# Moving the recurrence's input loads from SyncE's queue to GpSimd's queue in a two-layer FoX / RWKV-7 trunk

## The chip, the cores and the metric

The kernel runs on one core of one Trainium2 chip. The metric is the device time of one execution in microseconds (us). Times come from several runs of the same program; beside them stands one profiled execution, whose trace gives the start and length of each instruction on each engine: TensorE (PE, with its weight loads as PEld), VectorE (DVE), ScalarE (ACT), GpSimd (POOL) and SyncE (SP). SP computes nothing here. It only issues DMA transfers, one after the other, and an issue whose wait is not yet fulfilled holds up all issues behind it.

## The reference, cut to what matters

Input and output are 1024 tokens by 1024 channels in float32. Layer 0 is a forgetting attention with a pooling mixer and a SwiGLU feed-forward (FFN). Layer 1 is an RWKV-7 time mixing and another SwiGLU FFN. The change touches only the recurrence of layer 1:

```
r = (xr @ w_r); k = (xk @ w_k); v = (xv @ w_v)
w = -softplus(-(w0 + tanh(xw @ w1) @ w2)) - 0.5
a = sigmoid(a0 + (xa @ a1) @ a2);  g = sigmoid(xg @ g1) @ g2
kk = heads(k * k_k); kk = kk / max(|kk|, 1e-12)
k = k * (1 + (a - 1) * k_a);  decay = exp(-exp(w))
for each token:                      # 16 heads, a 64 x 64 state each
    sa = state @ (-kk)
    state = state * decay + sa (kk * a)^T + v k^T
    y = state @ r
y = groupnorm(y) * ln_w + ln_b + sum(r * k * r_k) * v
out = (y * g) @ w_o
```

## The kernel before

Activations lie transposed: 128 channels on the partitions, 512 tokens (one "half") along the row, so one tile is 128x512 float32, 256 KB. Every large product is computed with both operands split into a rounded high part and a low rest, as three matmuls (L163 to L165). A weight chunk is therefore loaded raw (`wraw`, L150, issued by SP), cast to its high part by ACT (`whi`, L151), and DVE subtracts to get the low part (`wlo`, L152). There are two raw buffers (`k.rawbufs` is 2), so a raw load waits until the `wlo` of the chunk two places back is done.

The dense part of RWKV (`dense`, L811) computes r, k, v, s (the argument of the decay), a and g of each block of 128 channels and spills them to DRAM through ACT's queue (L799). Four "jobs" then run the recurrence: `job(grp, half)` (L983) takes four channel blocks ("pairs", as each holds two heads) of one half. Its parts are:

- the preparation, for each of the four pairs: load s, k, a, r, v (L1004, L1019, L1034, L1043, L1048, all through `load`, L955), build the factors on DVE and ACT, and multiply on PE (L1025, L1056, L1070, L1081). r, multiplied, is stored to DRAM as c (L1049);
- a triangular solve on DVE (L1092 to L1116: transposes, then 30 steps of L1106 and L1108) and PE (L1126, L1136); POOL's small fills (`ep` L1007, `XR` L1091, `nu` L1100) and copies (`Pc` L1017) belong to it;
- the recurrence over eight chunks of 64 tokens (L1151 to L1189). Beside it `bonus` (L973) loads c and v again and stores b;
- the end, for each pair: load b and g (L1214, L1215), normalise, store y (L1220).

That makes 36 loads a job: 20 + 8 + 8, and 144 in the four jobs. All go into one ring of seven tiles, `ld` (`rw.ld_bufs` is 7), so a load waits for the last reader of the tile loaded seven places earlier.

Beside the jobs runs a filler that keeps PE busy: while jobs (0,0) and (1,0) run, it is the second half's FFN of layer 0; while jobs (0,1) and (1,1) run, it is the first half's FFN of layer 1 (the matmuls `fm`). `weave` (L217) interleaves the two when the program is written. The order in which instructions stand in each engine's queue is then fixed at build time by a scheduler, which places instructions by priority and by its own model of when inputs are ready. At run time every engine takes its queue strictly in that order.

In the profiled execution job (0,0) prepares from about 1047 to 1125 us, job (1,0) from 1270 to 1357, job (0,1) from 1775 to 1862 and job (1,1) from 1998 to 2089.

Of the kernel before, what the change touches and what calls it, by code (L numbers as in the profile page):

```python
# [113 lines left out]
def nm(k, s):  # L114
    k.uid += 1
    return f"{s}_{k.uid}"
# [625 lines left out]
class Rwkv:  # L742
# [211 lines left out]

    def load(self, n):  # L955
        t = self.cp.tile([P, HN], F32, tag="ld", name=nm(self.k, "ld"), bufs=self.ld_bufs)
        self.k.nc.sync.dma_start(t, self.dt(n))
        return t

    def await_(self, n):  # L960
# [591 lines left out]
```

## Time and profile before

| | us |
|---|---|
| median of 3 runs | 2701.37 |
| lowest and highest run | 2699.15 and 2703.07 |
| the profiled execution | 2699.03 |
| span of its trace, first to last instruction | 2697.2 |
| mean granted TensorE clock | 0.993 of full speed |
| bytes moved by DMA | 307 MB, 114 GB/s on average |

The profile has a page (busy time of each engine, the chain of work that ended last, groups of instructions) and views that answer questions about a stretch: who waited for whom, busy time by stretch, instructions in order of time. In a row of the timeline stand start, length, engine, line, operation, output and inputs, and in brackets the idle time before it with what ended it. "SPq" is SP's queue of DMA issues. In the order of time, SP's row shows an issue, not the transfer.

### The profile page before, as it was taken

The numbers are of one execution on the slowest core, as the hardware profiler recorded it, in microseconds if no ns is written. First come the engines' busy times: TensorE is split into PE (matmuls) and PEld (weight loads), VectorE is DVE, ScalarE is ACT, GpSimd is POOL, SyncE is SP. The second block draws the span as 40 slices with busy tenths as digits, with TensorE's granted clock in tenths as the row PEclk, the third lists the DMA queues.
The fourth block names the chain that finished last, engine by engine and source line by source line (L and its number), as shares of the span: only waits on it lengthen the run. The fifth ranks groups of instructions, "written<-read, shape, count | busy, mean of one in ns | idle before, by whom it ended". The sixth has DMA issues, their size and how long they took to land.

```text
span 2697.2 us, 40269 instructions
## 1 busy us (share of the span) xinstructions
PE 2633.8 (98%) x15368; PEld 2080.5 (77%) x15368; DVE 1724.3 (64%) x2940; ACT 1301.9 (48%) x2299; POOL 50.6 (2%) x139
## 2 busy tenths in 40 slices
PE   8999999999999999999999999999999999999999
PEld 6787878788888777777777677777777778888887
DVE  8777684654446655975995685469768856634443
ACT  7555564442224765534634466664445444332232
POOL 1000000000001000000000000000000000000000
PEclk9999999999999999999999999999999999999999
DMA  4111131233333546424523534454344336333333
GB/s 136 58 52 55 44 98 48 83 97 96 96 98 114 168 162 191 129 82 123 160 87 100 194 101 161 160 182 128 91 141 134 93 100 199 109 98 94 98 98 94
DMA packets 170817, 307.03 MB, mean 114 GB/s; under 512 B 18928, under 2 KB 25968, under 8 KB 170624
## 3 DMA queue, kind: packets, MB, share of 16 engines
q1 hardware_dynamic: 156800, 279.29, 33.6%
q10 hardware_dynamic: 13824, 25.17, 2.5%
q8 instruction: 120, 1.97, 0.3%
q14 instruction: 73, 0.60, 0.1%
HBM read 257.96 MB, written 46.43 MB: 113 GB/s over the span
## 4 chain that ended last, share of the span: by engine, by line
PE 77%; DVE 14%; DMA 3%; ACT 3%; issue 2%; SPq 0%; DVEq 0%; ACTq 0%
PE mm L163 16%; PE mm L164 16%; PE mm L165 16%; PE fm L163 6%; PE fm L164 5%; PE fm L165 5%; DVE wlo L152 2%; PE mm L175 1%; DVE nu L1108 1%; DVE pd L1106 1%; DMA wraw<-in_wu_dram 1%; DVE ZL L1064 1%; ACT whi L151 1%; PE o L1173 1%; PE s L1161 1%
## 5 line engine op out<-in xcount | busy, mean ns | idle before, releaser
L151 ACT CAST whi<-wraw 128x512 fp32r<-128x512 f32 x738 | 453.7, 617 | 867.4 <-PE mm L164 478.7
L152 DVE TENSOR_TENSOR wlo<-wraw,whi 128x512 fp32r<-128x512 f32 x738 | 501.3, 684 | 449.6 <-ACT whi L151 441.1
L163 PE MATMUL mm<-hh,whi 128*128 128x512 f32 x864 | 344.1, 400 | 6.2 <-ACT hh L355 6.1
L165 PE MATMUL mm<-hh,wlo 128*128 128x512 f32 x864 | 338.4, 392 | 0.0
L164 PE MATMUL mm<-hl,whi 128*128 128x512 f32 x864 | 337.9, 392 | 0.0
L163 PE MATMUL mm<-uh,whi 128*128 128x512 f32 x728 | 283.6, 391 | 0.9 <-DVE x L1317 0.9
L165 PE MATMUL mm<-uh,wlo 128*128 128x512 f32 x728 | 283.1, 390 | 1.0 <-DVE wlo L152 1.0
L164 PE MATMUL mm<-ul,whi 128*128 128x512 f32 x728 | 283.2, 390 | 0.0
L163 PE MATMUL fm<-h1h,whi 128*128 128x512 f32 x528 | 220.2, 417 | 14.8 <-DVE sg L726 9.9
L164 PE MATMUL fm<-h1l,whi 128*128 128x512 f32 x528 | 210.3, 398 | 0.1
L165 PE MATMUL fm<-h1h,wlo 128*128 128x512 f32 x528 | 209.5, 397 | 0.5 <-DVE wlo L152 0.5
L163 PEld LDWEIGHTS mm<-hh,whi 128*128 128x128 f32 x864 | 162.3, 188 | 43.4 <-ACT hh L355 7.8
L165 PEld LDWEIGHTS mm<-hh,wlo 128*128 128x128 f32 x864 | 162.5, 188 | 34.4 <-issue 0.2
L164 PEld LDWEIGHTS mm<-hl,whi 128*128 128x128 f32 x864 | 162.7, 188 | 33.1 <-DVE hl L260 1.7
L163 PE MATMUL fm<-hh,whi 128*128 128x512 f32 x416 | 170.9, 411 | 3.3 <-ACT hh L259 2.3
L164 PE MATMUL fm<-hl,whi 128*128 128x512 f32 x416 | 164.9, 396 | 0.2 <-DVE hl L260 0.2
L165 PE MATMUL fm<-hh,wlo 128*128 128x512 f32 x416 | 164.6, 396 | 0.0
L163 PEld LDWEIGHTS mm<-uh,whi 128*128 128x128 f32 x728 | 136.5, 188 | 34.6 <-issue 3.5
L164 PEld LDWEIGHTS mm<-ul,whi 128*128 128x128 f32 x728 | 136.6, 188 | 30.9 <-issue 1.1
L165 PEld LDWEIGHTS mm<-uh,wlo 128*128 128x128 f32 x728 | 136.7, 188 | 30.1 <-DVE wlo L152 1.8
L705 DVE TENSOR_TENSOR x<-mm,x 128x512 f32<-128x512 f32 x96 | 66.3, 692 | 119.3 <-PE mm L165 119.2
L163 PEld LDWEIGHTS fm<-h1h,whi 128*128 128x128 f32 x528 | 100.6, 191 | 47.1 <-DVE sg L726 12.2
(338 smaller groups left out, 4645.4 us busy)
## 6 DMA issues: line engine op xcount, KB each, us to landing
wraw<-in_wg_dram SPq DMA_DIRECT2D x176, 256.0 KB, 2.8
wraw<-in_wu_dram SPq DMA_DIRECT2D x176, 256.0 KB, 2.7
wraw<-in_wd_dram SPq DMA_DIRECT2D x176, 256.0 KB, 2.7
wraw<-in_w_in_dram SPq DMA_DIRECT2D x52, 256.0 KB, 2.9
x<-in_xT_dram SPq DMA_DIRECT2D x32, 256.0 KB, 4.6
x<-x SPq DMA_DIRECT2D x32, 256.0 KB, 3.3
wraw<-in_w_k_dram SPq DMA_DIRECT2D x32, 256.0 KB, 2.8
wraw<-in_w_v_dram SPq DMA_DIRECT2D x32, 256.0 KB, 3.0
```

The source lines that it names most:

```text
L151: k.nc.scalar.copy(hi[0:p, 0:n], raw[0:p, 0:n])
L152: k.nc.vector.tensor_tensor(lo[0:p, 0:n], raw[0:p, 0:n], rd(hi[0:p, 0:n]), ALU.subtract)
L163: nc.tensor.matmul(out, wh, xh, start=(first and i == 0), stop=False)
L164: nc.tensor.matmul(out, wh, xl, start=False, stop=False)
L165: nc.tensor.matmul(out, wl, xh, start=False, stop=(last and i == n - 1))
L175: k.nc.tensor.matmul(out[n * q:n * q + n], w[:, n * j:n * j + n], xs[j], start=c == 0, stop=c + g == len(xs), tile_position=(0, n * q))
L705: nc.vector.tensor_tensor(X[half][m], o, X[half][m], ALU.add)
L1064: nc.vector.tensor_tensor(ZL[h][HS[1 - h], i, bs], s4[HS[1]], self.msk[HS[1]].rearrange("p a t -> p (a t)").unsqueeze(1).broadcast_to([64, ...
L1106: nc.vector.tensor_tensor(pv, nu[:, j + 1:32, j:j + 1].broadcast_to([P, n, j]), nu[:, j:j + 1, 0:j].broadcast_to([P, n, j]), ALU.mult)
L1108: nc.vector.tensor_tensor(nu[:, j + 1:32, 0:j], nu[:, j + 1:32, 0:j], pv, ALU.add)
L1161: nc.tensor.matmul(z[HS[h], i], ZL[h][:, i, c, 0:64], SV[h][:, i, c], start=True, stop=True)
L1173: nc.tensor.matmul(sp[HS[h], i], BK[h][:, i, c], uv[h][:, i], start=True, stop=True)
```

## The change

`load` issues its transfer from GpSimd's queue instead of SyncE's. Nothing else in the code differs.

```
     def load(self, n):
         t = self.cp.tile([P, HN], F32, tag="ld", name=nm(self.k, "ld"), bufs=self.ld_bufs)
-        self.k.nc.sync.dma_start(t, self.dt(n))
+        self.k.nc.gpsimd.dma_start(t, self.dt(n))
         return t
```

SP's queue goes from 1074 to 930 transfers; POOL's goes from 140 instructions to 284. The raw weights (L150) and all stores stay on SP. Since the scheduler places by its model, the orders on PE, DVE and ACT shift as well, in the jobs alone.

SP's queue early in job (0,0): `ld` is the ring tile, s0, k1, a1, r1, v1, s2, k2 are inputs of pairs 0 to 2, `wraw` a raw weight chunk of the filler, c0 the stored product of pair 0. Minus is before, plus after.

```order
-L957 DMA ld_2269_9653<-k1_0_7966 128x512
 L150 DMA wraw_2285_9714<-in_wu0_dram 128x512
 L150 DMA wraw_2295_9788<-in_wd0_dram 128x512
-L957 DMA ld_2272_9670<-a1_0_8592 128x512
+L150 DMA wraw_2300_9829<-in_wd0_dram 128x512
 L1049 DMA c0_0_9493<-ld_2241_9486 128x512
-L957 DMA ld_2275_9679<-r1_0_9030 128x512
-L957 DMA ld_2276_9684<-v1_0_8461 128x512
-L957 DMA ld_2302_9840<-s2_0_8120 128x512
-L957 DMA ld_2304_9848<-k2_0_8007 128x512
-L150 DMA wraw_2300_9829<-in_wd0_dram 128x512
```

The raw chunk 9829 stood behind six loads and one store; it now follows the chunk ahead of it directly.

POOL's queue at the end of job (0,0)'s preparation: c2, v2 and c3 are loads of `bonus`, XR and nu the tiles of the triangular solve that POOL fills.

```order
+L957 DMA ld_2564_11299<-c2_0_9881 128x512
+L957 DMA ld_2565_11301<-v2_0_8502 128x512
 L1091 MEMSET XR_2220_9416 32x32x32 x2
+L957 DMA ld_2602_11507<-c3_0_10070 128x512
 L1100 MEMSET nu_2367_10216 128x16x16
 L1100 MEMSET nu_2367_10216 128x2x8x8
```

The load of c3 has come between the fills of XR and those of nu, and it waits there for its ring tile.

PE's queue early in job (1,0): `fm` is a filler matmul, t the product of L1025 for the second pair.

```order
 L164 MATMUL fm_2709_11984<-h1l_2553_11242,whi_2706_11978 128x512
-L165 MATMUL fm_2709_11984<-h1h_2552_11241,wlo_2707_11979 128x512
-L163 MATMUL fm_2709_11984<-h1h_2593_11487,whi_2706_11978 128x512
-L164 MATMUL fm_2709_11984<-h1l_2594_11488,whi_2706_11978 128x512
-L165 MATMUL fm_2709_11984<-h1h_2593_11487,wlo_2707_11979 128x512
-L163 MATMUL fm_2709_11984<-h1h_2638_11716,whi_2706_11978 128x512
-L164 MATMUL fm_2709_11984<-h1l_2639_11717,whi_2706_11978 128x512
-L165 MATMUL fm_2709_11984<-h1h_2638_11716,wlo_2707_11979 128x512
-L163 MATMUL fm_2709_11984<-h1h_2687_11877,whi_2706_11978 128x512
-L164 MATMUL fm_2709_11984<-h1l_2688_11878,whi_2706_11978 128x512
-L165 MATMUL fm_2709_11984<-h1h_2687_11877,wlo_2707_11979 128x512
 L1025 MATMUL t_2721_12069<-kn_2720_12067,cc_58 128x512
```

The ten filler matmuls have moved behind the job's product: the second pair's L1025 and the L1056 matmuls after it now come ten matmuls earlier in PE's order.

More of the change, by code (lines that the diff above doesn't have):

```diff
@@ L956, in load @@
         t = self.cp.tile([P, HN], F32, tag="ld", name=nm(self.k, "ld"), bufs=self.ld_bufs)
-        self.k.nc.sync.dma_start(t, self.dt(n))
+        self.k.nc.gpsimd.dma_start(t, self.dt(n))
         return t
```

## The prediction

> **What bounds the kernel now.** I read the busy times first, then the chain that ended last, then the busy time by stretch for the parts of the program in which the recurrence's loads occur.
>
> ```profile
> span 2697.2 us, 40269 instructions
> PE 2633.8 (98%) x15368; PEld 2080.5 (77%) x15368; DVE 1724.3 (64%) x2940; ACT 1301.9 (48%) x2299; POOL 50.6 (2%) x139
> ...
> PE 77%; DVE 14%; DMA 3%; ACT 3%; issue 2%; SPq 0%; DVEq 0%; ACTq 0%
> ```
>
> PE is busy for 98% of the span and carries 77% of the chain. No change of a queue can gain more than PE's idle time, and only the part of it that falls into the jobs. The stretches below are, in turn, preparation and recurrence of jobs (0,0), (1,0), (0,1) and (1,1); the columns are the length of the stretch, then busy time on PE, PEld, DVE, ACT and POOL, then granted clock, DMA share and GB/s.
>
> ```profile
> 1000.00:1130.00 130.00, 125.87 (x750) 98.45 (x751) 90.90 (x145) 72.95 (x130) 6.08 (x20) 0.99 0.51 159
> 1130.00:1260.00 130.00, 124.52 (x1267) 96.67 (x1265) 87.53 (x165) 53.19 (x103) 0.00 (x0) 0.97 0.32 96
> 1260.00:1360.00 100.00, 95.78 (x635) 72.63 (x633) 89.11 (x138) 58.45 (x105) 5.21 (x18) 0.98 0.48 149
> 1360.00:1490.00 130.00, 125.45 (x1290) 97.76 (x1288) 89.67 (x171) 54.20 (x105) 0.53 (x1) 0.99 0.33 99
> ...
> 1734.00:1864.00 130.00, 124.63 (x747) 98.09 (x745) 92.10 (x143) 78.38 (x141) 6.07 (x19) 0.99 0.51 165
> 1864.00:1990.00 126.00, 123.72 (x1277) 94.78 (x1277) 88.85 (x170) 49.51 (x97) 1.01 (x2) 0.99 0.32 96
> 1990.00:2090.00 100.00, 94.61 (x619) 73.25 (x619) 88.45 (x133) 57.74 (x104) 4.64 (x16) 0.98 0.47 148
> 2090.00:2240.00 150.00, 146.75 (x1377) 113.08 (x1376) 105.06 (x199) 65.17 (x124) 0.00 (x0) 0.99 0.35 108
> ```
>
> PE's idle time is length minus busy: 4.13, 4.22, 5.37 and 5.39 us in the preparations, 19.1 together, and 5.48, 4.55, 2.28 and 3.25 in the recurrences, 15.6 together. So 34.7 us, 1.3% of the time, is the most that can be won. In the two preparations that start right after another job DVE is busy for 89% and 88% of the stretch: there DVE sets the pace, and its work does not change.
>
> **What goes: the loads in SP's queue.** These are SP's own waits, with total us, times, and the longest.
>
> ```profile
> SPq L150 <- DVE wlo L152: 1564.0, 647, 23.5
> ...
> SPq L957 <- DVE bk L1040: 36.3, 16, 5.1
> ...
> SPq L957 <- PE o L1081: 32.0, 10, 8.8
> ...
> SPq L957 <- DVE kn L1030: 22.2, 9, 6.6
> ...
> SPq L957 <- DMA c<-ld: 19.7, 15, 2.5
> ```
>
> The four largest waits of loads (L957) come to 110.2 us in which no raw weight behind them could be issued. But SP waits 1564 us for `wlo` anyway, which frees the raw buffers, so most raw loads have no buffer to go to when a load blocks them. Whether the blocked ones matter is read at PE:
>
> ```profile
> L165 PE MATMUL fm<-h1h,wlo 128*128 128x512 f32 x528 | 209.5, 397 | 0.5 <-DVE wlo L152 0.5
> ```
>
> In 528 filler matmuls that read `wlo`, PE stood still 0.5 us for it. What remains is the detour: a late raw chunk makes ACT wait at its cast, and ACT and DVE take the job's work behind it in order. A place where it happens is at the end of the second preparation:
>
> ```profile
> 1343.37 0.32 SPq L957 DMA_DIRECT2D ld<-c  x1
> 1343.97 0.33 SPq L150 DMA_DIRECT2D wraw<-in_wu_dram  x1
> ```
>
> The raw chunk goes out 0.60 us after the load ahead of it. I take one such place that reaches PE in each of the four preparations: 4 x 0.60 = **-2.4 us**. From the one side it is 0, as PE's own row has it, and from the other the 19.1 us of idle time in the preparations.
>
> **What comes: the same loads from POOL.** No DMA is issued from POOL in this trace, so its cost is bounded by the nearest rows. On SP an issue and its landing look like this, with the engines that stood idle for a load.
>
> ```profile
> L957 SPq DMA_DIRECT2D ld<-v x32: 319/410/1052, 1049.5 to 2154.3; - x32
> ...
>   ACT kp L1036: 2.6, 2
>   ACT kn L1021: 1.5, 1
>   DVE ZL L1045: 0.5, 1
> ...
> DMA to landing us min/median/max: 2.5/2.9/6.1
> ```
>
> Of 144 loads four were waited for by an engine, 4.6 us in all; the others land while DVE and ACT still work on the pair before. How much later, L, does a load land when POOL issues it? The nearest rows are POOL's own instructions beside a busy DVE.
>
> ```profile
> 1053.58 0.20 POOL L1017 COPY Pc<-ep 128x8 f32<-128x8 f32 x1 [17.02 <-ACT ep L1008]
> ...
> 1063.99 1.12 POOL L1017 COPY Pc<-ep 128x8 f32<-128x8 f32 x1 [2.83 <-ACT ep L1008]
> 1075.76 0.11 POOL L1007 MEMSET ep<- 128x8 f32 x1 [10.64 <-DVE ld L1046]
> ```
>
> ```profile
> 1064.37 0.68 DVE L152 TENSOR_TENSOR wlo<-wraw,whi 128x512 fp32r<-128x512 f32 x1
> 1064.97 0.73 DVE L1032 SCALAR_TENSOR_TENSOR ZL<-kn,cv,ep 64x512 f32<-64x512 f32 x1
> ```
>
> The same copy takes 0.20 us, or 1.12 us while DVE runs one instruction after the other; the fill takes 0.11 us, and the DVE instructions beside the slow copy keep their 0.68 and 0.73 us. So DVE can hold POOL up, POOL does not hold up DVE, and L is 0.92 us if issuing behaves like the slow copy, and 0 if it behaves like the fill. The far end is 6.1 - 2.9 = 3.2 us, the slowest landing against the median one. Below nothing it can reach -4.6 us in all, if POOL issues so early that the four waits go. I take L = 0.92, the slow copy, since it is the row in which POOL meets the DVE of the preparation, at the four loads waited for: 4 x 0.92 = **+3.7 us**. At the far end I count two loads a job, as the second pair's first loads are nearly as tight: 8 x 3.2 = +25.6 us.
>
> The Trainium skill speaks to this choice. Its page SBUF — State Buffer, section Who interferes with whom, says that a DVE instruction with two SBUF inputs holds up only those GpSimd instructions that read SBUF, and it infers that writing DMA descriptors needs the write side alone. The trace agrees as far as it goes: the copy that reads was slowed, the fill that only writes was not. By that rule L from this cause is 0, the term is 0, and the whole sum below would be -1.3 in place of +2.4. Its page DMA: Bandwidth & Descriptors, section Specifications, gives a first byte after about 1 us from GpSimd and 0.6 us from sync; an estimate from these is 4 x 0.4 = 1.6 for the term and +0.3 for the sum. No row of this trace shows either figure.
>
> **What moves on POOL.** Loads wait for their ring tile, and POOL's fills now stand behind them. The tight place is the load of c3, which waits for the last L1081 and stands ahead of the fills of nu:
>
> ```profile
> 2084.82 1.15 PE L1081 MATMUL o<-cc,ld 64*64 64x64 f32 x32
> ```
>
> ```profile
> 2088.80 0.68 POOL L1100 MEMSET nu<- 128x256 f32 x5 [7.93 <-DVE nu L1095]
> ```
>
> The tile is free at 2085.97 and the fill started at 2088.80, so POOL has 2.8 us for one issue. Against 0.41 us on SP, or 1.12 us for the slowest copy, this is cover enough: **0 us**. Without that cover the DVE steps L1106 and L1108, which are in series, would start later in each job by what the issue exceeds 2.8 us.
>
> **What moves on PE, ACT and DVE.** The clearest place is early in job (1,0). The rows are of PE, and then of ACT.
>
> ```profile
> 1286.32 0.39 PE L164 MATMUL fm<-h1l,whi 128*128 128x512 f32 x1
> 1286.55 0.39 PE L165 MATMUL fm<-h1h,wlo 128*128 128x512 f32 x1
> 1287.29 1.13 PE L1025 MATMUL t<-kn,cc 128*128 128x512 f32 x2 [0.35 <-ACT kn L1021]
> ...
> 1290.13 0.70 PE L1070 MATMUL o<-cc,bk 64*128 64x64 f32 x11
> 1292.68 1.12 PE L1056 MATMUL s<-ZL,bk 64*128 64x128 f32 x6 [1.86 <-DVE ZL L1064]
> ```
>
> ```profile
> 1284.79 0.62 ACT L151 CAST whi<-wraw 128x512 fp32r<-128x512 f32 x1
> ...
> 1285.98 0.63 ACT L725 ACTIVATE sg<-sg 128x512 f32<-128x512 f32 x1
> 1286.52 0.72 ACT L1021 ACTIVATE kn<-ld,cv 128x512 f32<-128x512 f32 x1
> ```
>
> Filler matmuls follow each other by 0.23 us (1286.55 - 1286.32). Ten of them now stand behind L1025, so PE reaches it 2.3 us earlier. On ACT the cast of 1284.79 and L725 now stand behind L1021, which makes kn earlier by 0.62 + 0.63 = 1.25 us at best. The 0.35 us wait thus grows by about 1.1 us. The 1.86 us wait at L1056 stays: three of the moved matmuls, 0.7 us, now stand ahead of the group that waits, but the L1070 group of 0.70 us that stood there has gone behind it. Net **+1.1 us**, with bounds of -2.2 (both waits gone) and +2.3 (nothing earlier on ACT). The other shifts are by a few rows each way; I count them at 0.
>
> **Sum.** -2.4 + 3.7 + 0 + 1.1 = +2.4 us. On the profiled execution's own 2699.03 (2697.2 of span and 1.8 around it) that gives 2701.4. The median of the runs stands 2.3 above that execution, so in the measure of the runs it is **2703.8 us**. A measurement of this kernel can tell about 0.2%, 5.4 us, from no change.
>
> **The rivals.** Faster: with SP free, raw chunks come one place earlier throughout, ACT and DVE stop idling at casts, and the preparations pack. Price: half of the 19.1 us, -9.6, which gives 2691.8. For it speak the 110.2 us of blocked SP; against it, the 0.5 us at PE and a DVE busy for 89% of the preparation with work that stays.
>
> Slower: loads from POOL land later, and the first ones of each job and the second pair's set the preparation back. Price: 8 loads x L - 1.3, the other terms of the sum; with all eight tight it decides from L = 0.84, where it passes 5.4 us. With L = 2.0, about midway between the copy's 0.92 and 3.2, it is +14.7, or 2716. For it: DVE has no reserve in the preparation, so a late start is not made up. Against it: only four loads of 144 were waited for.
>
> Slower by another way: DVE starves POOL's issues or c3 holds the fills of nu beyond 2.8 us; at two DVE instructions of 0.7 us more for each of the 8 tight loads that is +11.2, or 2713. For it: the copy that took 1.12 us. Against it: the fill of 0.11 us in a stretch with as busy a DVE, and the 2.8 us of cover. The Trainium skill's page SBUF — State Buffer, section SBUF: two separate sides, tells of such starving where DVE runs a copy in a two-port mode; no row quoted here is one.
>
> That the change does nothing it says can be excluded for the queues, since the 144 loads do stand in POOL's; but they may be hidden on both queues alike, which is the forecast.
>
> **How the numbers follow.** Forecast 0.42; its own range is 2696 to 2707. Packing 0.26. Later landing 0.24, starving 0.08. Faster 0.26, same 0.42, slower 0.32. The range that leaves no more than 2 in 10 out goes from 2689, two thirds of the idle time in the preparations, to 2720, L = 2.5 at the eight tight loads.
>
> **What would show it.** If the forecast is right, PE's idle time in the eight stretches stays near 34.7 us and engines wait under 10 us in all for `ld`. If packing is right, the preparations' idle time falls below 12 us and ACT's waits for raw chunks shrink. If later landing is right, the landing time of L957 rises by 1 us or more and L1021, L1036 and L1045 wait for it. If the fills are late, L1100 starts well after the second transpose L1095. I am wrong altogether if DVE's instructions get longer beside POOL's issues, or if stretches without any job change.

## The result, and the profile after

| | before | after |
|---|---|---|
| median of the runs taken together (4 each), us | 2700.66 | 2719.12 |
| lowest and highest, us | 2699.15 and 2703.07 | 2716.68 and 2720.90 |
| span of the profiled execution, us | 2697.2 | 2714.9 |
| mean granted TensorE clock | 0.993 | 0.990 |

The ratio is 1.0069, with a 95% interval of 1.0057 to 1.0082: the change costs 18.6 us (0.0069 x 2700), against a forecast of +2.4. The time lies inside the range, near its upper end, and near the price of the rival "later landing" (2716). That it falls there is luck, as the experiments show: the range was drawn for loads that land late, and the new order of instructions costs as much without a single load on POOL.

The page after, in the same lines as before: span, busy times, shares of the chain.

```profile
span 2714.9 us, 40415 instructions
PE 2637.8 (97%) x15368; PEld 2083.8 (77%) x15368; DVE 1725.2 (64%) x2940; ACT 1299.9 (48%) x2299; POOL 128.4 (5%) x283
...
PE 75%; DVE 14%; DMA 5%; ACT 4%; issue 2%; SPq 0%; ACTq 0%; DVEq 0%; POOLq 0%; POOL 0%
```

The same 15368 matmuls take 4.0 us more (2637.8 against 2633.8), and PE stands still for 77.1 us in place of 63.4, which is 13.7 more; together 17.7, the difference of the spans. DVE's busy time is as it was. So only POOL has more to do; PE waits more, and its matmuls get a little longer. DMA's share of the chain went from 3% to 5%.

Where it happens, by the same eight stretches (length; busy PE, PEld, DVE, ACT, POOL; clock, DMA share, GB/s):

```profile
1000.00:1131.50 131.50, 124.93 (x746) 96.92 (x745) 89.62 (x142) 71.82 (x129) 19.61 (x44) 0.99 0.49 154
1131.50:1262.00 130.50, 124.43 (x1285) 96.70 (x1285) 88.72 (x169) 54.54 (x106) 5.29 (x10) 0.99 0.32 99
1262.00:1367.00 105.00, 96.19 (x608) 72.70 (x607) 90.32 (x140) 58.63 (x106) 19.84 (x44) 0.95 0.47 143
1367.00:1495.00 128.00, 125.19 (x1295) 97.80 (x1294) 87.78 (x167) 52.88 (x102) 4.29 (x8) 1.00 0.32 97
...
1739.00:1871.00 132.00, 124.99 (x753) 98.07 (x752) 91.94 (x143) 78.81 (x142) 20.03 (x44) 0.99 0.51 160
1871.00:1997.00 126.00, 123.56 (x1277) 94.76 (x1277) 89.00 (x170) 49.51 (x97) 5.30 (x10) 0.99 0.31 96
1997.00:2101.00 104.00, 95.86 (x618) 73.81 (x618) 88.62 (x134) 58.03 (x105) 18.76 (x42) 0.97 0.46 143
2101.00:2257.00 156.00, 148.94 (x1378) 114.44 (x1377) 105.69 (x198) 64.22 (x122) 5.55 (x11) 0.98 0.34 104
```

Length minus PE's busy time adds up to 48.9 us where before had 34.7: all of the added idle time lies in the jobs, none in the stretches without one. DVE's sum over the eight is 731.69 against 731.67. The loads themselves:

```profile
L957 POOL DMA_DIRECT2D ld<-v x32: 536/536/545, 1043.3 to 2171.4; - x32
...
  ACT kn L1021: 4.9, 3
  ACT kp L1036: 2.6, 4
  DVE ld L1005: 0.8, 1
  DVE ZL L1045: 0.3, 1
...
DMA to landing us min/median/max: 2.8/3.3/8.6
```

An issue on POOL takes 0.536 us (the first figures of a row are min/median/max in ns), a load lands after 3.3 us in the median instead of 2.9, and engines wait 8.6 us for loads instead of 4.6. These are waits of ACT and DVE, so the 4.0 us between them are at most 4.0 of the 18.6. Most of it must have another cause.

To see where the time goes, I cut both traces at the same instructions of each job: the first L1021, the fill of nu (L1100), the first L1163 and the last L1218. "Preparation" runs from the first to the second of these, "solve" from the second to the third. After minus before, in us:

| start of (0,0) | preparation (1,0) | preparation (0,1) | preparation (1,1) | solve (1,1) | all else | last L1218 |
|---|---|---|---|---|---|---|
| +1.6 | +3.8 | +2.1 | +2.9 | +5.7 | +1.0 | +17.1 |

Between traces in which nothing was changed in a stage I found differences up to about 2 us, so only the larger of these can be read alone. The solve of (1,1) stands out, and no load of the preparation is in it.

### The profile page after: what moved, and what is told of

It reads as the page before. It is cut to its first block, busy times and chain, and to the rows that moved or that the text cites. A ratio compares the mean times of both kernels' runs of the same rounds, so it can differ in the third digit from the quotient of the medians.

```text
span 2714.9 us, 40415 instructions
## 1 busy us (share of the span) xinstructions
PE 2637.8 (97%) x15368; PEld 2083.8 (77%) x15368; DVE 1725.2 (64%) x2940; ACT 1299.9 (48%) x2299; POOL 128.4 (5%) x283
## 4 chain that ended last, share of the span: by engine, by line
PE 75%; DVE 14%; DMA 5%; ACT 4%; issue 2%; SPq 0%; ACTq 0%; DVEq 0%; POOLq 0%; POOL 0%
PE mm L163 16%; PE mm L164 16%; PE mm L165 16%; PE fm L163 6%; PE fm L164 5%; PE fm L165 5%; DVE wlo L152 3%; DVE nu L1108 1%; DVE pd L1106 1%; PE mm L175 1%; DMA wraw<-in_wg_dram 1%; DMA wraw<-in_wd_dram 1%; ACT whi L151 1%; DMA wraw<-in_wu_dram 1%; PE o L1173 1%
```

## Experiments: the queue and the order apart

The change does two things: the 144 loads go out from another queue, and the scheduler, which places by its model of the queues, writes another order for all engines. The build can record an order and place a program by a recorded one, so the two can be varied apart. One list holds 24,875 instructions of all engines, and each engine takes its own from it. On PE, DVE and ACT the two orders differ mainly in five pieces: the preparation of (0,0) (from position 9295), preparation and solve of (1,0) (11650 to 12972), shorter stretches early in (0,1) and early in (1,1), and the end of the preparation and the solve of (1,1) (19531 to 20170). The edit common to all, shortened:

```
-        self.k.nc.sync.dma_start(t, self.dt(n))
+        q = self.queues.get(n[0], self.queues["*"])
+        getattr(self.k.nc, q).dma_start(t, self.dt(n))
```

`queues` maps the first letter of an input to an engine. In one run it maps the whole name, and in two runs the v that `bonus` loads has a letter of its own, `u`. A build with one mapping records an order (ORDER), and the kernel is built by that order with its own mapping (RUN). Differences in us below are the ratio minus 1, times 2700; each ratio compares with runs of the kernel before on the same chip. The expectations go by medians instead, where the first run below is 9 us above the kernel before.

### Each order on each queue

The order of before, all loads on POOL:

```
+ORDER = {"*": "sync"}
+RUN = {"*": "gpsimd"}
```

> The loads are issued from POOL, as in the changed kernel, but PE, DVE and ACT keep the order of instructions of the kernel before. Theory A (landing: loads that are issued just before they are needed land later from POOL, and POOL's queue holds them behind its own fills and copies): most of the 18.5 us stays, 2711 to 2718 us, with PE idle 10 us or more above the kernel before in the four preparations. Theory B (order: the scheduler's other order on PE, DVE and ACT costs the time, the queue nothing): 2699 to 2705 us.

The order of the changed kernel, all loads on SP:

```
+ORDER = {"*": "gpsimd"}
+RUN = {"*": "sync"}
```

> The loads are issued from SP as before, but PE, DVE and ACT keep the order of instructions of the changed kernel. Theory A: within 5 us of the kernel before, 2697 to 2706 us. Theory B: 2714 to 2722 us. If both have a part, the longer solve of job (1,1), 5.7 us, belongs to the order and shows here (2704 to 2710 us) and not in the run with the order of before.

| order of | loads on | ratio, 95% | us |
|---|---|---|---|
| before | POOL | 1.0045 [1.0032, 1.0057] | +12.2 |
| changed kernel | SP | 1.0075 [1.0062, 1.0087] | +20.2 |
| changed kernel | POOL (the change) | 1.0069 [1.0057, 1.0082] | +18.6 |

Neither cause stands alone, and they don't add up. The new order without a single load on POOL costs as much as the whole change, and the new queue without the new order costs two thirds of it. Put the other way round, the queue adds nothing that can be told from zero once the new order is there (18.6 against 20.2), and 12.2 us where it is not.

### Which loads

With the order of before, k and a alone (32 loads) on POOL, and then the other 112 alone:

```
+RUN = {"*": "sync", "k": "gpsimd", "a": "gpsimd"}
```

> Order of instructions of the kernel before; only the loads of k and a (32 of 144) are issued from POOL, the others from SP. In the trace of before these two are issued 3 to 6 us ahead of their first reader, hardly more than the 2.9 us that they take to land. Theory A: these 32 carry most of what all 144 cost, at least two thirds of the run with all loads on POOL. If every load costs alike, 32/144, a fifth of it: about 3 us. Theory B: nothing, 2699 to 2705 us.

```
+RUN = {"*": "gpsimd", "k": "sync", "a": "sync"}
```

> Order of instructions of the kernel before; all loads but those of k and a (112 of 144) are issued from POOL. Theory A: little, 2699 to 2706 us, as s, r, v, c, b and g are issued 5 to 20 us ahead of their readers. If every load costs alike, four fifths of the run with all loads on POOL. If POOL's waits hold its own fills and copies, L1100 or L1017 starts later and the time shows here: 2706 to 2712 us.

k and a: 1.0010 [1.0001, 1.0019], +2.7 us. The others: 1.0044 [1.0031, 1.0056], +11.9 us, as much as all 144 together. The guess that most of the cost sits at k and a, which are the loads that L1021 and L1036 wait for, was wrong; 2.7 is about their share by number, 32 of 144.

### Where the order costs

Here pieces of one order are put into the other: `rows` is the order that is kept, `two` the one that gives the piece.

```
+for a, b in PARTS:
+    rows[a:b] = two[a:b]
```

First the changed kernel, all loads on POOL, with before's order in the solve of (1,1) alone; then in addition in the whole of (1,0) up to its recurrence (with before's tile addresses); then before, all loads on SP, with the changed kernel's order in the solve of (1,1) alone.

```
+PARTS = [(19531, 20170)]
```

> The changed kernel (all loads on POOL, its own order), but with the order of before in one piece: the end of the preparation and the triangular solve of job (1,1). Theory B (order): the solve of job (1,1), which took 64.0 us from the fill of nu to the first L1163 against 58.3 before, is back near 58.3, and the time falls by about 5.5 us, to 2713 to 2715 us. Theory A (queue): the solve stays near 64 us and the time at 2717 to 2721 us.

```
+PARTS = [(11650, 12813), (12872, 12932), (12932, 12972), (19531, 20170)]
```

> The changed kernel, with the order of before in two pieces: all of job (1,0) up to its recurrence, and the solve of job (1,1). Theory B: both pieces give back what the two orders differ by in the traces, 3.8 to 5.3 us in the preparation of job (1,0) and 5.5 us in the solve, less 1.4 us in the solve of job (1,0): 2708 to 2712 us, the time of the order of before on POOL (2710). Theory A: 2716 us or more.

```
+ORDER, OTHER = {"*": "sync"}, {"*": "gpsimd"}
+PARTS = [(19531, 20170)]
+RUN = {"*": "sync"}
```

> The kernel before (loads on SP, its own order), but with the order of the changed kernel in one piece, the solve of job (1,1). Theory B: the solve takes about 64 us and the time rises by about 5.5 us, to 2705 to 2708 us, with no load on POOL. Theory A: 2699 to 2703 us.

| kernel | ratio, 95% | us |
|---|---|---|
| changed, before's order in the solve of (1,1) | 1.0048 [1.0035, 1.0061] | +13.0 |
| changed, before's order in (1,0) too | 1.0023 [1.0014, 1.0032] | +6.2 |
| before, changed order in the solve of (1,1) | 1.0023 [1.0012, 1.0033] | +6.2 |

The piece of order around the solve of (1,1) is worth 5.6 us where it is taken away (18.6 - 13.0, two intervals that overlap) and 6.2 where it is put in, without any load on POOL. The piece of (1,0) is worth another 6.8 (13.0 - 6.2); it was only taken away, and together with before's tile addresses. The lengths of the two stages in the traces, in us, follow the order and not the queue:

| stage | before's order there | the new order there |
|---|---|---|
| preparation of (1,0) | SP: 78.6, 78.3; POOL: 77.1, 77.0 | SP: 81.9; POOL: 82.3, 83.1 |
| solve of (1,1) | SP: 58.3; POOL: 58.2, 58.1, 58.3 | SP: 63.3, 63.7; POOL: 64.0 |

So with the loads on POOL these two pieces carry some 12 of the 18.6 us. It does not follow that the order costs 12 and the queue the rest: with before's order in all pieces the loads on POOL cost 12.2 us, which is 6.0 more than with before's order in these two alone. The other three pieces of the new order, then, seem to help when the loads are on POOL (or the addresses do); they were not tried apart. With the loads on SP, where the new order costs 20.2, the traces show most of what is left in the preparations of (0,1) and (1,1), 6.1 and 6.0 us longer than before; no run took these apart either.

What the order did in the solve of (1,1) can be read from the rows. DVE before, at the end of the 30 steps:

```profile
2121.17 0.69 DVE L152 TENSOR_TENSOR wlo<-wraw,whi 128x512 fp32r<-128x512 f32 x1
2121.78 0.18 DVE L1108 TENSOR_TENSOR nu<-nu,pd 128x30 f32<-128x30 f32 x1
2122.00 1.98 DVE L1116 STREAM_TRANSPOSE t<-nu 128x1024 f32<-128x1024 f32 x1
```

DVE after:

```profile
2131.94 0.19 DVE L1108 TENSOR_TENSOR nu<-nu,pd 128x30 f32<-128x30 f32 x1
2132.16 2.14 DVE L1116 STREAM_TRANSPOSE t<-nu 128x1024 f32<-128x1024 f32 x1
2134.34 1.94 DVE L1114 STREAM_TRANSPOSE XR<-nu 32x1024 f32<-32x1024 f32 x1
2136.31 0.69 DVE L726 TENSOR_TENSOR sg<-fm,sg 128x512 f32<-128x512 f32 x1
2137.03 2.02 DVE L1114 STREAM_TRANSPOSE XR<-nu 32x1024 f32<-32x1024 f32 x1
2139.09 1.29 DVE L152 TENSOR_TENSOR wlo<-wraw,whi 128x512 fp32r<-128x512 f32 x2
```

One `wlo` stood ahead of the last L1108; now two stand together behind three transposes of 2 us. `wlo` is what frees a raw buffer, so the next raw load goes out late. ACT after:

```profile
2142.64 0.62 ACT L151 CAST whi<-wraw 128x512 fp32r<-128x512 f32 x1 [6.45 <-DMA wraw<-in_wd_dram]
2143.84 0.62 ACT L259 CAST gh<-sg 128x512 fp32r<-128x512 f32 x1 [0.58 <-DVE sg L732]
2144.49 0.57 ACT L121 COPY XR<-s 32x512 f32<-32x512 f32 x1
```

ACT waits 6.45 us for that raw chunk, and the job's own copies (L121), which the solve's next matmuls need, stand behind the cast in ACT's queue. In the kernel that has only this piece of the new order and every load on SP, DVE's rows stand in the same sequence, and ACT shows the same wait:

```profile
2133.61 0.62 ACT L151 CAST whi<-wraw 128x512 fp32r<-128x512 f32 x1 [6.35 <-DMA wraw<-in_wd_dram]
```

And with before's order put back in the changed kernel (the second kernel of the table), the waits of ACT in this stage read 2.4 us for `wd`, the figure that before has too. The chain from the one `wlo` to the copy is read from the traces; a kernel that moves that row alone was not tried. In (1,0) PE's waits grew; after, then before:

```profile
PE t L1025 <- ACT kn L1021: 3.8, 2, 2.3
PE s L1056 <- DVE bk L1040: 2.7, 1, 2.7
```

```profile
PE s L1056 <- DVE bk L1040: 1.1, 1, 1.1
...
PE t L1025 <- ACT kn L1021: 0.4, 1, 0.4
```

With before's order put back in (1,0), the wait at L1025 is 1.8 us and that at L1056 for `bk` 1.2.

### What the queue costs

All five kernels here keep the order of before. The first has every load on POOL, but POOL's copies (Pc) and fills (ep), behind which loads stood, go to ACT and DVE:

```
-nc.gpsimd.memset(ep[:, :, 0:1], 1.0)
+nc.vector.memset(ep[:, :, 0:1], 1.0)
-nc.gpsimd.tensor_copy(Pc[:, :, i:i + 1], ep[:, :, 64:65])
+nc.scalar.copy(Pc[:, :, i:i + 1], ep[:, :, 64:65])
```

> All loads on POOL with the order of before, but POOL's copy of Pc (L1017, 16 times) is done by ACT and its fill of ep (L1007) by DVE, so that no load stands behind a copy that waits for ACT. Theory A1 (loads are held in POOL's queue behind its own waiting copies, as the second s of job (0,0), issued 7.9 us later than on SP): most of the 9 us between the order of before on POOL (2710) and on SP (2701) goes: 2701 to 2705 us. Theory A2 (a load from POOL lands later, or takes bandwidth from raw weights that it shared a queue with): 2708 to 2713 us.

Then the 80 loads of the preparations on POOL; the 64 of bonus and end; the first five of job (0,0); b and g of the ends:

```
+RUN = {"*": "sync", "s": "gpsimd", "k": "gpsimd", "a": "gpsimd", "r": "gpsimd", "v": "gpsimd"}
```

> Order of instructions of the kernel before; only the 80 loads of the preparations (s, k, a, r, v) are issued from POOL, the 64 of the bonus and of the end (c, v, b, g) stay on SP. With all 144 on POOL in this order the time was 2710 us, 9 us above before. Theory A2 (loads of the preparation that are needed soon land 0.3 to 0.5 us later and are issued one by one in 0.54 us): two thirds or more of it, 2706 to 2711 us, in the preparations of jobs (0,1) and (1,1) and at the start of job (0,0). Theory A3 (the loads of the bonus and the end wait on POOL for a store to land and hold the next job's first loads): 2700 to 2704 us.

```
+RUN = {"*": "sync", "c": "gpsimd", "u": "gpsimd", "b": "gpsimd", "g": "gpsimd"}
```

> Order of instructions of the kernel before; only the 64 loads of the bonus and of the end of a job (c, v, b, g) are issued from POOL. Theory A2: 2700 to 2704 us. Theory A3: two thirds or more of the 9 us, 2706 to 2711 us, at the end of the jobs and the start of the next one.

```
+RUN = {"*": "sync", "s0_0": "gpsimd", "k0_0": "gpsimd", "a0_0": "gpsimd", "r0_0": "gpsimd", "v0_0": "gpsimd"}
```

> Order of instructions of the kernel before; only the first five loads of job (0,0), s0, k0, a0, r0 and v0, are issued from POOL, the other 139 from SP. With all 80 loads of the preparations on POOL, job (0,0) started 3.9 us later: the five no longer stand behind a raw weight chunk in one queue but are under way beside it. Theory A4 (the queue was also an order of precedence among transfers): these five alone bring most of that, the first L1021 2.5 to 4 us later and 2702 to 2705 us. Theory A5 (later loads bring it, or the start differs by itself from run to run): the first L1021 within 1 us of before and 2699 to 2702 us.

```
+RUN = {"*": "sync", "b": "gpsimd", "g": "gpsimd"}
```

> Order of instructions of the kernel before; only the 32 loads of b and g at the end of the jobs are issued from POOL. With c, v, b and g on POOL the time was 5 us above before, 1.2 us of it between job (0,1) and the first load of job (1,1) and 2.2 and 2.4 us in the preparations of jobs (0,1) and (1,1). If b and g bring it (each b load waits for a store to land, and the end of a job then frees tiles later for the next one): 2703 to 2706 us. If c and v bring it: 2699 to 2702 us.

| on POOL, order of before | ratio, 95% | us |
|---|---|---|
| all 144, POOL's copies and fills elsewhere | 1.0035 [1.0021, 1.0049] | +9.4 |
| 80 of the preparations | 1.0034 [1.0022, 1.0047] | +9.2 |
| 64 of bonus and end | 1.0019 [1.0008, 1.0030] | +5.1 |
| the first five | 1.0012 [1.0003, 1.0021] | +3.2 |
| b and g | 1.0013 [1.0003, 1.0022] | +3.5 |

With POOL freed, 9.4 us of 12.2 stay, within the intervals of one another: loads held behind POOL's copies can't be told from nothing. The two groups of loads give 9.2 and 5.1, which is 14.3 against 12.2 for both, again within the intervals. Whether b and g or c and v bring the 5.1 stays open, as 3.5 and 5.1 are within each other's intervals. Five loads alone bring about a third of the preparations' share (3.2, interval 0.8 to 5.7), and here a mechanism can be seen. Rows of SP before, at the start of (0,0):

```profile
1045.35 0.33 SPq L150 DMA_DIRECT2D wraw<-in_wu_dram  x1
...
1047.66 0.38 SPq L957 DMA_DIRECT2D ld<-s  x1
```

With the five on POOL (rows of POOL, then of SP):

```profile
1042.28 0.54 POOL L957 DMA_DIRECT2D ld<-k  x1 [5.54 <-PE mm L165]
...
1043.88 0.54 POOL L957 DMA_DIRECT2D ld<-v  x1
```

```profile
1045.94 0.33 SPq L150 DMA_DIRECT2D wraw<-in_wu_dram  x1
```

On SP the raw chunk stood ahead of the five loads. From POOL k to v, 256 KB each, are issued 2 to 4 us ahead of it, and they take 5.3, 6.4, 7.1 and 7.8 us to land, so all four are still under way when it goes out; the last lands at 1051.65. ACT before, and then with the five on POOL:

```profile
1050.23 0.60 ACT L151 CAST whi<-wraw 128x512 fp32r<-128x512 f32 x1
...
1053.36 0.71 ACT L1021 ACTIVATE kn<-ld,cv 128x512 f32<-128x512 f32 x1
```

```profile
1052.15 0.62 ACT L151 CAST whi<-wraw 128x512 fp32r<-128x512 f32 x1 [2.30 <-DMA wraw<-in_wu_dram]
1054.67 0.63 ACT L1008 ACTIVATE ep<-ld 128x512 f32<-128x512 f32 x1 [1.89 <-DVE ld L1005]
1055.20 0.71 ACT L1021 ACTIVATE kn<-ld,cv 128x512 f32<-128x512 f32 x1
```

The cast waits 2.30 us for the raw chunk where it waited for nothing before, and L1021, which stands behind it, comes 1.84 us later. That is less than the 2.5 to 4 us that were expected, and 0.59 of it is there already when the raw chunk is issued (1045.94 against 1045.35); the cast itself comes 6.21 us after that issue instead of 4.88. These five loads are there in time; it is the weight behind them that is late. The same cast waits 2.1 to 3.0 us in all five kernels with the 144 loads on POOL, in either order, and for nothing in before, in the two kernels above with every load on SP, and in the two that issue only loads of bonus and end from POOL.

For the later loads this does not carry over. With before's order and all 144 loads on POOL, these instructions waited for loads (us, times):

```profile
  ACT kp L1036: 7.4, 4
  ACT kn L1021: 3.7, 2
  DVE ZL L1045: 1.9, 1
  DVE ld L1005: 0.8, 1
```

That adds up to 13.8 us, 9.2 more than the 4.6 of before, while ACT's waits for raw chunks in the jobs stay as they were in sum (130.4 us against 132.5). So with before's order it is the waits for late loads that grew; how much of them reaches the span was not tested. With the changed kernel's order and every load on SP the same view gives 8.5 us (4.2 + 2.4 + 1.9): the 8.6 of the changed kernel belong to its order, and the queue adds 0.1 there. No run of these beat the kernel before.

## Why the prediction was right or wrong, by its own steps

**The bound.** That PE is the bound held, and so did the reading that a gain can only come from its idle time in the jobs: the loss came as idle time there too, 34.7 to 48.9 us.

**Term one, -2.4 us, raw chunks no longer blocked by loads:** the gain did not come. The row that sized it was misread. The raw chunk that goes out at 1343.97 was not held by the load 0.60 us ahead of it: its buffer came free when this `wlo` ended, at 1343.95.

```profile
1343.26 0.69 DVE L152 TENSOR_TENSOR wlo<-wraw,whi 128x512 fp32r<-128x512 f32 x1
```

With before's order and the loads on POOL, SP's wait for `wlo` rose from 1564.0 to 1675.6 us, and ACT's waits for raw chunks in the jobs stayed (130.4 us against 132.5). At the start of (0,0) the sign is even the other way: SP's single queue had kept the loads behind a raw chunk, and from two queues that chunk is 2.30 us late at its cast. With before's order the queue costs 12.2 us in all; what belongs to which of the later loads stays open.

**Term two, +3.7 us, later landing at the four loads waited for:** the waits rose by 4.0, but that agreement is luck. The same order with all loads on SP waits as long, 8.5 us, and with before's order, for which the term was worked out, the waits rose by 9.2. L is 0.4 us and not 0.92, by the medians, and eight or nine loads are waited for in place of four. The Trainium skill's page DMA: Bandwidth & Descriptors, section Specifications, gives first bytes of about 1 us from GpSimd and 0.6 from sync, a difference of 0.4. The trace agrees in size: the medians from issue to landing, 2.9 and 3.3 us, differ by 0.4.

**Term three, 0, the fills of nu:** right. The fill starts 2.2 us after the second L1095 in both traces.

**Term four, +1.1 us, the order on PE, ACT and DVE:** the step that failed most. I worked out one place and wrote that the other shifts "are by a few rows each way; I count them at 0". Beside the queue they are worth some 12 us: 6.8 in the piece of (1,0), from which the 1.1 was taken, and 5.6 to 6.2 in the solve of (1,1), which I did not look at, since hardly a load stands in it. A few rows are enough if one of them frees a buffer and three transposes of 2 us stand next to it.

**No term at all** was the clock. 4.0 of the 17.7 us of span are longer matmuls (below).

**The rivals.** Packing did not come: ACT's waits for raw chunks in the jobs grew from 132.5 to 156.0 us. Later landing had the price (2716) but not the size of its mechanism: eight tight loads by L = 0.4 are 3.2 us, and in the changed order the queue adds 0.1 us to the waits for loads. With before's order, where the queue adds 9.2, it may be much of the queue's cost. Starving did not come: POOL's issues take 0.536 us in the median, and DVE's instructions keep their times. Of the signs that I named, "engines wait under 10 us for `ld`" came true at 8.6, while PE's idle time in the jobs did not stay: the two signs that I had tied to one case came apart, a hint that the loads were not the main part.

## What to carry to other kernels

Where a scheduler places the program, an edit of a queue also draws a new order, and that can be worth more than the edit; hold the order fixed and vary the queue, then the other way round, before either is believed. In a comparison of two orders, rows that free a buffer (here `wlo`) are to be looked for first, and in every stage in which the orders differ, not only where the edited instructions stand. A queue shared by urgent and other transfers is also their precedence, and taking the others out can let them go ahead of the urgent ones, as at the start of (0,0). And a wait that grows after a change is not yet caused by it: here the same wait stood in the same order without the change.

## What the runs showed of the hardware

PE pauses can be paid for twice. The spans are cut here into windows of 3.41 us, the length of the shortest stretches at half clock. These are of after, around the late raw chunk of the solve of (1,1) (columns as above):

```profile
2150.90:2154.31 3.41, 0.80 (x24) 0.58 (x24) 2.51 (x4) 3.36 (x7) 0.00 (x0) 1.00 0.30 84
2154.31:2157.73 3.42, 3.13 (x44) 2.33 (x45) 1.66 (x4) 0.57 (x2) 0.00 (x0) 0.50 0.22 68
2157.73:2161.14 3.41, 3.41 (x9) 2.64 (x9) 1.15 (x2) 0.34 (x1) 0.00 (x0) 0.50 0.05 14
2161.14:2164.55 3.41, 3.41 (x29) 2.61 (x28) 1.66 (x3) 0.62 (x1) 0.00 (x0) 1.00 0.21 59
```

PE is still for 2.61 us of the first window at full clock; then the granted clock is 0.50 for two windows though PE is busy again. The same in before, after a pause of 1.70 us in a window:

```profile
1064.50:1067.90 3.40, 1.70 (x17) 1.27 (x11) 3.34 (x6) 3.32 (x8) 0.61 (x1) 1.00 0.75 225
1067.90:1071.30 3.40, 3.40 (x37) 2.94 (x36) 3.30 (x7) 2.35 (x5) 0.00 (x0) 0.51 0.06 18
```

A pause of that size does not always do it: from 1163.51 to 1166.93 in before PE is still for 1.75 us, and the next window has the full clock. In all the clock stood at half for 37.5 us before, 51.2 after, and 75.1 with the changed order on SP, where PE's busy time is 2647.8 us, 14.0 more than before. There the clock is the larger part of the 23.9 us by which that span is longer. The Trainium skill's page TensorE: Matmul & The Clock Gate, section Part 1: The HAM clock gate, has the clock fall after at least one idle window of about 3.4 us. The window's length and the half clock agree with the rows; that a whole window must be idle does not, since 1.7 and 2.6 us of one were enough here.

The issue on POOL was steady beside a busy DVE: 536 or 537 ns in the median for each kind of load, and 716 at the longest. The five first loads landed in 4.4 to 7.8 us from POOL, median 6.4, and in 2.8 to 5.7 from SP in the kernel before, median 4.2, against medians of 3.1 and 2.9 over all loads of the same two kernels. So the first ones are slower from either queue; whether the rest is the queue or what else is under way, these runs don't tell.
